# Attention scores as two full-height products over stacked query halves, with three fill steps ahead of them

## Chip, core and metric

The kernel runs on one core of a Trainium2 chip. The metric is the device time of one execution in microseconds (us), here the median of several executions. A core has a matrix engine (TensorE, in the profile PE, with its weight loads as PEld), a vector engine (VectorE, DVE), a scalar engine (ScalarE, ACT), a general engine (GpSimd, POOL), and a sync engine that issues most transfers (SyncE, SP). Each engine runs its own instructions in program order and waits for the others by semaphores. POOL issues transfers too, between its other work.

## Reference

Two layers of a hybrid backbone over 512 latent tokens and 256 context tokens of width 1024. Each layer projects its input once, gives the parts to three mixers (a state-space scan, a two-dimensional Fourier mixer and neighbourhood attention with 6 heads of width 64), joins them by one output projection, and ends in a gated feed-forward. The change is in the attention's scores:

```python
def na_latent(q, k, v, kc, vc, rpb):
    ...
        s_win = jnp.einsum('bqhd,bwqkhd->bhqwk', q_row, k_win).astype(jnp.float32) * scale + bias[None]
        s_win = s_win.reshape(B, H, GRID_W, nwin)
        s_ctx = jnp.einsum('bqhd,bchd->bhqc', q_row, kc).astype(jnp.float32) * scale
        p = jax.nn.softmax(jnp.concatenate([s_win, s_ctx], axis=-1), axis=-1).astype(q.dtype)
    ...

def na_context(qc, kc, vc):
    ...
    s = jnp.einsum('bqhd,bkhd->bhqk', qc, kc).astype(jnp.float32) * d ** -0.5
```

Queries and keys of the latent tokens are rotated by their grid position before. The context's own attention (`na_context`) is needed in the first layer only.

## The kernel before

Every float32 matrix product is done as three products of halves: a value is split into a high part (a rounded copy) and a low part (the rest), and high·high, high·low and low·high are added up in PSUM. Names that end in h and l, or the indices 0 and 1, are the two halves.

**Layer.** The input projection (`w_in`, L600) fills tiles for the scan, the Fourier mixer and, through `rope` (L697 on), rotated queries and keys, which SP writes to DRAM as `qd` and `kd` (head row, half, token). Beside it runs the state-space scan (`ssm`), in 12 units per layer: a scan on DVE (L746), products with tables on POOL (L749 to L759), output products on PE (L768 to L773). Then comes the value projection (`w_v`, L648), and then attention woven with a fill.

**Attention** works on three pairs of heads. `attn_load` (L939) brings in a pair's keys `kt` (128 rows: two heads of 64; both halves; 768 tokens), its queries `ql` (both halves, 512 latent tokens) and, in the first layer, `qc` (256 context tokens), all by transfers that POOL issues (L946, L947, L951). Two pairs are loaded at once; the third when the second has reached its second step. The queries' buffers are slices of one `u` tile, which the scan's tables use before.

A step is one block of 128 queries of a pair: `scores` (L998 on) calls `both` twice per step, for a window of 256 latent keys and for the 256 context keys; with three products for two heads that makes 12 matmuls of 64 rows by 128 columns with 256 moving columns. In the first layer a fifth step per pair, `scores_ctx`, scores the context queries. So there are 5 steps per pair in the first layer and 4 in the second, 27 in all and 324 such matmuls (L996). The softmax follows on DVE (L1017: add the bias, row minimum; L1041, L281: normalise) and ACT (L1019: exponential). One step later PE transposes the probabilities (L1053, 128x128), ACT copies them back (L1055), and PE multiplies them with the values (L1068 in 128x64 tiles, L1078 for the context).

**Order.** `weave` interleaves attention's generator with a fill by the two numbers that it is given: in both layers the Fourier mixer `fnet` (L860 its small tables, L870 `pz`, L875 `three`, L833 its output) and the gated unit of the scan (`glu`), and in the first layer products with modulation weights too (`mod`, L167, weights by L165). Within that code order a scheduler decides each engine's order ahead of the run. The program's instruction list on an engine is then fixed.

The lines that matter below, before and after the change:

| work | before | after |
|---|---|---|
| scores products | L996 | L1014, L1015 |
| loads of keys / queries / context queries | L947 / L946 / L951 | L956, L962 (low half) / L953 / L968 |
| scan: tables' products on POOL | L749 to L759 | L755 to L765 |
| scan: output products on PE | L768, L771, L773 | L774, L777, L779 |
| fnet: tables, `pz`, `three` | L860, L870, L875 | L866, L876, L881 |
| bias on POOL | L1008 | L1027 |
| transposes / values | L1053 / L1068 | L1072 / L1087 |

Of the kernel before, what the change touches and what calls it, by code (L numbers as in the profile page):

```python
# [8 lines left out]
F32 = mybir.dt.float32  # L9
F32R = mybir.dt.float32r  # L10
# [8 lines left out]
NL, NC = 512, 256  # L19
# [15 lines left out]
class Builder:  # L35
# [59 lines left out]
    def consts(self):  # L95
        nc = self.nc
        self.cols = self.k("cols", [128, 8])
        nc.sync.dma_start(self.cols, self.ap["cols"])
        self.ident = self.k("ident", [128, 128])
        self.nidx = self.k("nidx", [128, 96])  # L100
        self.later = self.k("later", [128, 96])
        self.b0 = [self.k(f"b0{i}", [128, 4, 32]) for i in range(2)]
        self.eye16 = self.k("eye16", [128, 16])
        self.junk = self.k("junk", [128, 512], mybir.dt.bfloat16)
        self.zero = self.k("zero", [1, 128], mybir.dt.bfloat16)
        nc.vector.memset(self.zero, 0.0)
        self.sgn, self.nsgn, self.sgn2pi, self.halfpi = (self.cols[:, i:i + 1] for i in range(4))
        self.mhalf = self.cols[:, 4:5]
        self.qd = [self.dram(f"qd{l}", [NH * HD, 2, NT]) for l in range(DEPTH)]
        self.kd = [self.dram(f"kd{l}", [NH * HD, 2, NT]) for l in range(DEPTH)]  # L110
        self.ud = [self.dram(f"ud{l}", [G, HC, 8, 128]) for l in range(DEPTH)]
        self.zd = [self.dram(f"zd{l}", [G, HC, 8, 96]) for l in range(DEPTH)]
        self.tabd = [self.dram(f"tabd{l}", [NU, 2, 128, 1792]) for l in range(DEPTH)]
        self.wd = [self.dram(f"wd{l}", [NU, 128, 240]) for l in range(DEPTH)]
        self.gd = [self.dram(f"gd{l}", [4, DM]) for l in range(DEPTH)]
        self.rbd = [self.dram(f"rbd{l}", [NH, 16, 8, 384]) for l in range(DEPTH)]
        self.xd = [self.dram(f"xd{l}", [6, 128, DM]) for l in range(3)]
        self.decay = {}
        self.turn = [self.k(f"turn{l}", [128, 48]) for l in range(DEPTH)]
        self.rho = [self.k(f"rho{l}", [128, 48]) for l in range(DEPTH)]  # L120
        self.mcol = [[self.k(f"mc{l}{a}", [128, 2, 16]) for a in range(3)] for l in range(DEPTH)]
        self.gcol = [self.k(f"gcol{l}", [128, 2, 8]) for l in range(DEPTH)]
        self.amod = [[self.k(f"am{l}{i}", [128, 2, 8]) for i in range(2)] for l in range(DEPTH)]
        self.dcol = [self.k(f"dcol{l}", [128, NU]) for l in range(DEPTH)]
# [564 lines left out]
        self.fh[j], self.fl[j] = self.split2(eo, pc)  # L689

    def ev_q(self, l, j, pl, pc):
        self.rope(l, lambda i: self.qd[l][128 * j:128 * j + 128, i], pl, pc, -HD ** -0.5)

    def ev_k(self, l, j, pl, pc):
        self.rope(l, lambda i: self.kd[l][128 * j:128 * j + 128, i], pl, pc, 1.0)

    def rope(self, l, dst, pl, pc, scale):  # L697
        nc = self.nc
        if self.rc is None:
            self.rc, self.rs = self.s(), self.s()  # L700
            nc.sync.dma_start(self.rc, self.ap["rope"][:, 0, :])
            nc.sync.dma_start(self.rs, self.ap["rope"][:, 1, :])
        q, sh = self.s(), self.s()
        nc.scalar.activation(q, pl, AF.Copy, scale=scale)
        nc.vector.stream_shuffle(sh, q, [(i + 16) % 32 for i in range(32)])
        (nc.vector if l == 0 else nc.gpsimd).tensor_tensor(out=sh, in0=sh, in1=self.rs, op=ALU.mult)
        self.tt(q, q, self.rc, ALU.mult)
        self.tt(q, q, sh, ALU.add)
        parts = [(q, 0, NL)]
        if pc is not None:  # L710
            qc = self.c()
            nc.scalar.activation(qc, pc, AF.Copy, scale=scale)
            parts.append((qc, NL, NT))
        for x, a, b in parts:
            new = self.s if a == 0 else self.c
            hl = (new(F32R), new(F32R))
            self.split(*hl, x)
            for i in range(2):
                nc.sync.dma_start(dst(i)[..., a:b], hl[i].bitcast(F32))


    def ssm_scan(self, l, k, tab):
# [216 lines left out]
    def attn_load(self, l, hp):  # L939

        nc = self.nc
        last = l == DEPTH - 1
        kt = self.tab(F32R, (128, 2, NT))
        rows = slice(128 * hp, 128 * hp + 128)
        ql = self.Q[hp % 2]
        nc.gpsimd.dma_start(ql, self.qd[l][rows, :, 0:NL])  # L946
        nc.gpsimd.dma_start(kt, self.kd[l][rows])  # L947
        qc = None
        if not last:
            qc = self.QC[hp % 2]  # L950
            nc.gpsimd.dma_start(qc, self.qd[l][rows, :, NL:NT])  # L951
        rb = self.z_p.tile([128, 2, 384], F32, tag="z", name="rb")
        for e in range(2):  # L953
            nc.sync.dma_start(rb[:, e, :], self.rbd[l][2 * hp + e].rearrange("c r n -> (c r) n"))
        return kt, ql, qc, rb

    def attn(self, l):


        nc = self.nc  # L960
        last = l == DEPTH - 1
        ua = self.ua = self.ut(F32R)  # L962
        two = lambda a, n: ua[:, a:a + 2 * n].rearrange("p (i n) -> p i n", i=2)
        self.Q = [two(0, NL), two(2 * NL, NL)]
        if not last:
            qc = self.s(F32R)
            self.QC = [two(4 * NL, NC), qc.rearrange("p (i n) -> p i n", i=2)]
        self.extra = [ua[:, 4 * NL:5 * NL]] if last else []  # L968
        self.bm = [self.q() for _ in range(3)]
        for b in self.bm:  # L970
            nc.gpsimd.memset(b[:, 256:512], 0.0)
        self.mask = [self.c() for _ in range(3)]
        for ty in range(3):
            nc.sync.dma_start(self.mask[ty], self.ap["mask"][:, ty, :])
        self.kq = {hp: self.attn_load(l, hp) for hp in range(2)}
        steps = [(hp, i) for hp in range(3) for i in range(4 if last else 5)]
        pend = []
        self.nbm = 0
        for hp, i in steps:
            pend.append((hp, i, (self.scores if i < 4 else self.scores_ctx)(l, hp, i)))  # L980
            yield
            if len(pend) > 1:
                self.values(l, *pend.pop(0))
            for r in pend[-1][2]:
                self.normalise(*r)
            if i == 1 and hp == 1:
                self.kq[2] = self.attn_load(l, 2)
            yield
        self.values(l, *pend[0])

    def both(self, sp, q, k, qs, ks):

        for n, (a, b) in enumerate(((0, 0), (0, 1), (1, 0))):
            for e in range(2):
                r = slice(64 * e, 64 * e + 64)
                self.nc.tensor.matmul(sp[e], q[r, a, qs], k[r, b, ks], start=(n == 0), stop=(n == 2))  # L996

    def scores(self, l, hp, i):  # L998
        nc = self.nc
# [276 lines left out]
    def build(self):  # L1276
# [46 lines left out]
        for l in range(DEPTH):  # L1323
            last = l == DEPTH - 1
            self.yh, self.yl = [None] * 8, [None] * 8
            self.fh, self.fl = [None] * 2, [None] * 2
            self.rc = self.rs = None
            self.U = [None] * 3
            w = self.w_in(l, 0, 6, pre if l == 0 else None)
            ahead = (AHEAD0, 3)[l]  # L1330
            tables = (lambda k: self.prep_dir(0, big, k, True, "tt")) if l == 0 else (lambda k: self.tables(1, k))
            tabs = {k: tables(k) for k in range(ahead)}
            for _ in range(3):
                next(w)
            self.weave(self.ssm(l, tabs, tables, ahead), w, 13, 8)
            self.run(self.w_v(l))
            fill = self.fnet(l)
            if l == 0:
                mods = self.chain(self.mod(0, 1, "m", self.q), self.mod(0, 2, "m", self.q))
                fill = self.zip(fill, mods, 11, 18)  # L1340
            fill = self.chain(fill, [None] * (0, 4)[l], self.glu(l))
            self.weave(self.attn(l), fill, *((30, 33) if l == 0 else (24, 15)))
            pre_gu = self.gu_pre(l)
            if l == 0:
                ssm_a = self.scalars_load(1)
            self.w_out(l, self.ap["x"] if l == 0 else self.xd[2])
            if l == 0:
                new = lambda: self.xt1()[:, 0:512]
                self.ffn(l, pre_gu, fill=self.chain(self.prep(1, ssm_a), *(self.mod_ahead(1, a, new) for a in range(3))))
            else:  # L1350
                self.ffn(l, pre_gu, out=self.ap["out"])
# [112 lines left out]
```

## Time and profile before

| | |
|---|---|
| median of 3 runs | 1657.88 us (1656.64 to 1658.67) |
| the profiled execution | 1656.89 us |
| its span in the trace | 1655.1 us |
| mean granted TensorE clock in it | 0.982 of full speed |
| PE busy | 1591.4 us, 96% of the span |
| DVE, ACT, POOL busy | 60%, 40%, 14% |
| scores in the first layer | 237.26 us to about 332 us of the span |
| scores in the second layer | 1172.95 us to 1221 us of the span |

How to read the rows further down: times are us from the span's start. A line such as L996 is a line of the kernel before. In a timeline a row gives a start, a duration and a number of instructions (x12); neighbours of one kind are merged; an idle time before the row stands in brackets with what ended it. Matmuls are pipelined, so a row's duration overlaps the next row's start: what a group costs PE is read from its start to the next group's start. In rows of windows each engine has its busy time, PEclk is the granted TensorE clock as a share of full speed (1.00 is 2.4 GHz and 0.50 is 1.2 GHz), and DMA the mean busy share of the 16 DMA engines.

### The profile page before, as it was taken

What the parts mean: (1) busy time and instruction counts of PE and PEld (TensorE: products, weight loads), DVE (VectorE), ACT (ScalarE), POOL (GpSimd) and SP (SyncE); (2) the same over time, 40 slices, a digit from 0 to 9 for tenths busy, and PEclk for the clock granted to TensorE, in tenths of its full rate; (3) what the DMA queues carried; (4) which work ended last, traced back from release to release, by engine and by line L of the source; (5) the groups of instructions that cost most, each with busy time, mean ns of one, the idle gap of its engine ahead of it and who ended that gap; (6) DMA issues with size and microseconds to landing.
All of it is one profiled execution on the core that took longest, in us unless ns stands there. A gap on an engine that the chain in (4) does not pass through costs nothing. (4 is left out here: it accounts for less than half of the span.)

```text
span 1655.1 us, 23574 instructions
## 1 busy us (share of the span) xinstructions
PE 1591.4 (96%) x9097; PEld 1308.6 (79%) x9097; DVE 995.0 (60%) x1855; ACT 663.8 (40%) x1289; POOL 237.3 (14%) x268
## 2 busy tenths in 40 slices
PE   5998889999999999999999999989999999999997
PEld 1887776678988888778788788879777888888886
DVE  7699976765565656433343357697764534554455
ACT  6556655646556322211221138422564432222222
POOL 1000012002111233000000014375411100000002
PEclk8999899999999999999999999999899999999999
DMA  9444368634133424642524346476713322233222
GB/s 333 145 152 139 88 200 252 234 130 160 65 115 128 146 91 141 207 153 90 191 89 149 135 185 207 159 225 195 227 65 140 129 88 102 77 117 103 86 79 86
DMA packets 101391, 240.08 MB, mean 145 GB/s; under 512 B 25424, under 2 KB 56784, under 8 KB 88480
## 3 DMA queue, kind: packets, MB, share of 16 engines
q1 hardware_dynamic: 97968, 229.93, 40.9%
q0 software_dynamic: 3312, 8.65, 1.7%
q8 instruction: 71, 1.16, 0.3%
q14 instruction: 40, 0.33, 0.1%
HBM read 201.26 MB, written 38.47 MB: 145 GB/s over the span
## 5 line engine op out<-in xcount | busy, mean ns | idle before, releaser
L600 PE MATMUL b<-s,wh 128*128 128x512 f32 (+1 forms) x1856 | 552.0, 377 | 7.0 <-DVE c L572 5.3
L600 PEld LDWEIGHTS b<-s,wh 128*128 128x128 f32 x1856 | 338.4, 190 | 80.4 <-issue 10.2
L600 PE MATMUL b<-s,wl 128*128 128x512 f32 (+1 forms) x928 | 346.7, 375 | 1.5 <-DVE wl L572 1.5
L591 ACT ACTIVATE wh<-wr 128x1024 fp32r<-128x1024 f32 (+4 forms) x184 | 185.3, 1027 | 345.6 <-PE b L600 251.5
L572 DVE TENSOR_TENSOR wl<-wr,wh 128x1024 fp32r<-128x1024 f32 (+4 forms) x184 | 221.3, 1219 | 110.6 <-ACT wh L591 100.8
L284 DVE TENSOR_TENSOR q<-q,b 128x512 f32<-128x512 f32 x180 | 122.8, 685 | 165.7 <-PE b L1192 165.1
L600 PEld LDWEIGHTS b<-s,wl 128*128 128x128 f32 x928 | 175.5, 189 | 32.4 <-DVE wl L572 2.6
L600 PE MATMUL b<-c,wh 128*128 128x256 f32 x944 | 179.3, 285 | 0.3 <-ACT c L591 0.3
L600 PEld LDWEIGHTS b<-c,wh 128*128 128x128 f32 x944 | 151.5, 191 | 5.8 <-ACT c L591 0.5
L287 DVE SCALAR_TENSOR_TENSOR s<-s,b 128x512 f32<-128x512 f32 x88 | 60.3, 685 | 134.2 <-PE b L600 86.9
L1192 PE MATMUL b<-wh,tab 128*128 128x512 f32 x400 | 137.1, 393 | 0.0
L600 PE MATMUL b<-c,wl 128*128 128x256 f32 x472 | 133.2, 284 | 0.0
L1192 PE MATMUL b<-wh,s 128*128 128x512 f32 x384 | 130.1, 392 | 0.0
L600 PEld LDWEIGHTS b<-c,wl 128*128 128x128 f32 x472 | 90.3, 191 | 1.4 <-issue 0.2
L1192 PEld LDWEIGHTS b<-wh,tab 128*128 128x128 f32 x400 | 75.1, 188 | 19.1 <-ACT c L1169 2.5
L1192 PEld LDWEIGHTS b<-wh,s 128*128 128x128 f32 x384 | 72.1, 188 | 19.8 <-issue 2.5
L1192 PE MATMUL b<-wl,tab 128*128 128x512 f32 x200 | 78.4, 392 | 0.0
L1192 PE MATMUL b<-wl,s 128*128 128x512 f32 x192 | 74.8, 390 | 0.0
L1224 POOL TENSOR_TENSOR q<-q,g 128x512 f32<-128x512 f32 x10 | 13.9, 1391 | 366.8 <-ACT junk L522 366.8
L591 ACT ACTIVATE s<-s 128x512 fp32r<-128x512 f32 x43 | 26.9, 627 | 93.9 <-DVE s L287 52.8
L534 POOL TENSOR_TENSOR ss<-ss,cols 128x1 f32<-128x1 f32 x42 | 30.6, 730 | 190.6 <-DVE ss L287 190.0
L1169 ACT ACTIVATE s<-b 128x512 f32<-128x512 f32 x44 | 26.0, 590 | 78.2 <-PE b L600 78.1
(329 smaller groups left out, 2633.6 us busy)
## 6 DMA issues: line engine op xcount, KB each, us to landing
wr<-in_w_gu SPq DMA_DIRECT2D x44, 1024.0 KB
wmod<-in_w_mod SPq DMA_DIRECT2D x46, 512.0 KB
wr<-in_w_down SPq DMA_DIRECT2D x22, 1024.0 KB
wmod<-in_w_mod SPq DMA_DIRECT2D x16, 1024.0 KB
wr<-in_w_in SPq DMA_DIRECT2D x10, 1024.0 KB
u<-in_w_mod SPq DMA_DIRECT2D x18, 512.0 KB
wr<-in_w_out SPq DMA_DIRECT2D x8, 1024.0 KB
tab<-tabd SPq DMA_DIRECT2D x12, 640.0 KB
```

The source lines that it names most:

```text
L284: self.nc.vector.tensor_tensor(out=out, in0=a, in1=b, op=op)
L287: self.nc.vector.scalar_tensor_tensor(out=out, in0=a, scalar=s, in1=b, op0=op0, op1=op1)
L534: nc.gpsimd.tensor_tensor(out=ss[:, 3:4], in0=ss[:, 2:3], in1=self.mhalf, op=ALU.pow)
L572: (eng or self.nc.vector).tensor_tensor(out=lo, in0=x, in1=hi.bitcast(F32), op=ALU.subtract)
L591: ins = self.nc.scalar.activation(hi, x, AF.Copy)
L600: self.nc.tensor.matmul(out, a[k], h[k][v][:, cs], start=(k == 0 and i == 0), stop=(k == 7 and i == 2))
L1169: nc.scalar.activation(tmp[v], gp, AF.Tanh, scale=0.5)
L1192: nc.tensor.matmul(pd, a[v][:, cs], w[:, ds], start=(j == 0 and i == 0), stop=(j == n - 1 and i == 2))
L1224: (nc.gpsimd, nc.vector)[hf].tensor_tensor(out=oo[hf], in0=oo[hf], in1=gates[t // 4][:, hf * 512:(hf + 1) * 512], op=ALU.mult)
```

## The change

It has three parts.

1. **Layout and products.** `qd` becomes one block per head with the 64 high rows above the 64 low rows. A query tile then holds, per head, 128 rows: high on rows 0 to 63, low on rows 64 to 127. The keys' high half is loaded twice, onto rows 0 to 63 and rows 64 to 127, and so is the low half. One full-height matmul with the high keys gives high·high + low·high; a second with the low keys gives high·low + low·low. `both` thus issues 2 matmuls per head with 128 rows where it issued 3 with 64: 8 per step for 12, 216 in all for 324.
2. **Loads.** A pair's keys come by two transfers of 384 KB for the high half (L956) and four for the low half (L962: two of 256 KB into `s` tiles, two of 128 KB into `c` tiles) where there was one of 768 KB. With the queries' loads that makes 7 or 8 transfers per pair for 2 or 3, and 768 KB more.
3. **Order of the code.** Attention's generator yields once after its loads, and three steps of the fill are taken before the weave starts; the weave's numbers go from 30:33 to 30:30 and from 24:15 to 24:12.

```diff
     def ev_q(self, l, j, pl, pc):
-        self.rope(l, lambda i: self.qd[l][128 * j:128 * j + 128, i], pl, pc, -HD ** -0.5)
+
+        base = self.qd[l][2 * j]
+
+        def dst(i, a, b):
+            return bass.AP(tensor=base.tensor, offset=base.offset + i * HD * NT + a,
+                           ap=[[2 * HD * NT, 2], [NT, HD], [1, b - a]])
+        self.rope(l, dst, pl, pc, -HD ** -0.5)
...
         kt = self.tab(F32R, (128, 2, NT))
         rows = slice(128 * hp, 128 * hp + 128)
         ql = self.Q[hp % 2]
-        nc.gpsimd.dma_start(ql, self.qd[l][rows, :, 0:NL])
-        nc.gpsimd.dma_start(kt, self.kd[l][rows])
+        qs = self.qd[l][2 * hp:2 * hp + 2].rearrange("e r n -> r e n")
+        nc.gpsimd.dma_start(ql, qs[:, :, 0:NL])
+        for e in range(2):
+            base = self.kd[l][128 * hp + 64 * e:128 * hp + 64 * e + 64]
+            nc.gpsimd.dma_start(kt[:, e, :], bass.AP(tensor=base.tensor, offset=base.offset,
+                                                    ap=[[0, 2], [2 * NT, HD], [1, NT]]))
+        kl = [self.sc(F32R) for _ in range(2)]
+        for e in range(2):
+            base = self.kd[l][128 * hp + 64 * e:128 * hp + 64 * e + 64]
+            for x, a, b in ((kl[e][0], 0, NL), (kl[e][1], NL, NT)):
+                nc.gpsimd.dma_start(x, bass.AP(tensor=base.tensor, offset=base.offset + NT + a,
+                                               ap=[[0, 2], [2 * NT, HD], [1, b - a]]))
+        kt = (kt, kl)
...
+        yield
         for hp, i in steps:
...
-        for n, (a, b) in enumerate(((0, 0), (0, 1), (1, 0))):
-            for e in range(2):
-                r = slice(64 * e, 64 * e + 64)
-                self.nc.tensor.matmul(sp[e], q[r, a, qs], k[r, b, ks], start=(n == 0), stop=(n == 2))
+        kt, kl = k
+        v, c0 = (0, ks.start) if ks.start < NL else (1, ks.start - NL)
+        for e in range(2):
+            self.nc.tensor.matmul(sp[e], q[:, e, qs], kt[:, e, ks], start=True, stop=False)
+            self.nc.tensor.matmul(sp[e], q[:, e, qs], kl[e][v][:, c0:c0 + 256], start=False, stop=True)
...
-            self.weave(self.attn(l), fill, *((30, 33) if l == 0 else (24, 15)))
+            attn = self.attn(l)
+            for g in (attn, fill, fill, fill):
+                next(g)
+            self.weave(attn, fill, *((30, 30) if l == 0 else (24, 12)))
```

How this moves instructions is shown at three places. In these listings `tab` is a tile of high keys (before: of both halves), `s` and `c` hold low keys in the changed kernel, `u` holds queries (and, in the scan's rows of the second layer, the scan's tables).

PE at the start of the first layer's attention, before:

```order
L860 MATMUL b<-s 128x256 x2
L167 MATMUL b<-wmod,scT 32x512 x8
L860 MATMUL b<-s 128x256 x2
L996 MATMUL b<-tab,u 128x256 x12
L870 MATMUL b<-s 128x256 x3
```

and after:

```order
L866 MATMUL b<-s 128x256 x2
L167 MATMUL b<-wmod,scT 32x512 x8
L866 MATMUL b<-s 128x256 x2
L876 MATMUL b<-s 128x256 x3
L774 LDWEIGHTS zero
L774 MATMUL b<-zero 128x384
L777 MATMUL b<-q 128x96 x4
L876 MATMUL b<-s 128x256
L1014 MATMUL b<-tab,u 128x256
L1015 MATMUL b<-s,u 128x256
```

The first step's scores stand four `pz` matmuls and a scan unit's first four rows later, and a step is 8 matmuls in which high and low keys alternate.

PE at the start of the second layer's attention, before:

```order
L870 MATMUL b<-s 128x256 x23
L870 MATMUL b<-s 1x256 x6
L771 MATMUL b<-q,u 128x96
L773 MATMUL b<-U,q 128x96
...
L875 MATMUL b<-wh,s 128x260 x2
L875 MATMUL b<-wl,s 128x260
...
L875 MATMUL b<-wl,c 128x260
L996 MATMUL b<-tab,u 128x256 x30
```

and after:

```order
L774 LDWEIGHTS zero
L774 MATMUL b<-zero 128x384
L777 MATMUL b<-q,u 128x96 x4
L881 MATMUL b<-wh,s 128x260 x2
...
L881 MATMUL b<-wl,c 128x260
L777 MATMUL b<-q,u 128x96
L779 MATMUL b<-U,q 128x96
...
L1014 MATMUL b<-tab,u 128x256
L1015 MATMUL b<-s,u 128x256
```

The thirty `three` matmuls (L875, now L881) stood between the scan's last output products and the first scores; now they stand ahead of those output products, and the scores follow these directly.

POOL at the same place, before:

```order
L947 DMA tab<-kd_128 128x1536
L754 MEMSET q 128x4
L755 TENSOR_TENSOR q<-q 128x4x95
L947 DMA tab<-kd_128 128x1536
L749 TENSOR_TENSOR q<-q,tab 128x384
...
L759 TENSOR_TENSOR q<-q 128x4x31
L947 DMA tab<-kd_128 128x1536
L946 DMA u<-qd_126 128x2x512 x2
```

and after:

```order
L956 DMA tab<-kd_128 128x1x768 x2
L962 DMA c<-kd_128 128x1x256
L760 MEMSET q 128x4
L761 TENSOR_TENSOR q<-q 128x4x95
L956 DMA tab<-kd_128 128x1x768 x2
L755 TENSOR_TENSOR q<-q,tab 128x384
...
L962 DMA c<-kd_128 128x1x256 x2
L763 MEMSET q 128x4
L764 TENSOR_TENSOR q<-q 128x4x64
L765 TENSOR_TENSOR q<-q 128x4x31
L956 DMA tab<-kd_128 128x1x768 x2
L953 DMA u<-qd_126 128x2x512 x2
```

Two transfers stand inside the last scan unit's products and the keys' loads are two each. Seven more low loads stand about two scan units earlier; the third pair's remaining two come among the bias instructions of the stage.

## Rows read from the trace of the kernel before

**Rows 1.** The page's first part: busy time of each engine.

```profile
PE 1591.4 (96%) x9097; PEld 1308.6 (79%) x9097; DVE 995.0 (60%) x1855; ACT 663.8 (40%) x1289; POOL 237.3 (14%) x268
```

**Rows 2.** Windows: the attention of layer one and two in their undisturbed parts.

```profile
core 0: us, PE busy (x) PEld busy (x) DVE busy (x) ACT busy (x) POOL busy (x), PEclk, DMA share, GB/s
245.00:335.00 90.00, 89.38 (x698) 59.92 (x691) 61.22 (x162) 54.82 (x130) 15.89 (x21) 1.00 0.72 233
1189.60:1228.00 38.40, 38.30 (x330) 30.14 (x330) 27.98 (x80) 26.03 (x61) 8.93 (x12) 1.00 0.21 50
```

**Rows 3.** Timeline of PE: scores, transposes and values in the steady stage.

```profile
248.83 1.32 PE L996 MATMUL b<-tab,u 64*128 64x256 f32 x12
250.08 0.66 PE L1053 MATMUL b<-ident,q 128*128 128x128 f32 x4
250.70 0.97 PE L996 MATMUL b<-tab,u 64*128 64x256 f32 x6
251.60 0.66 PE L1053 MATMUL b<-ident,q 128*128 128x128 f32 x4
252.19 0.97 PE L996 MATMUL b<-tab,u 64*128 64x256 f32 x6
...
319.53 0.98 PE L996 MATMUL b<-tab,u 64*128 64x256 f32 x12
320.44 0.54 PE L1068 MATMUL b<-q,vb 128*64 128x128 f32 x5
...
1201.03 1.09 PE L1053 MATMUL b<-ident,q 128*128 128x128 f32 x8
1202.06 0.97 PE L996 MATMUL b<-tab,u 64*128 64x256 f32 x6
```

**Rows 4.** Timeline of PE: the layers' starts of attention, with full-height groups.

```profile
232.70 3.21 PE L167 MATMUL b<-wmod,scT 128*32 128x512 f32 x16 [2.86 <-ACT va L649]
...
240.24 2.74 PE L870 MATMUL b<-s 128*128 128x256 f32 x21
242.82 0.36 PE L771 MATMUL b<-q 128*128 128x96 f32 x2
...
1161.53 0.33 PE L768 MATMUL b<-zero 1*128 1x384 bf16 x1 [0.90 <-DVE z L287]
...
1167.91 0.48 PE L875 MATMUL b<-wh,s 128*128 128x260 f32 x2
...
1172.03 0.28 PE L875 MATMUL b<-wl,c 1*128 1x260 f32 x1
1172.95 0.97 PE L996 MATMUL b<-tab,u 64*128 64x256 f32 x12 [0.64 <-DMA u<-qd]
1175.74 4.20 PE L996 MATMUL b<-tab,u 64*128 64x256 f32 x18 [1.82 <-DVE am L1017]
```

**Rows 5.** Timeline of POOL: the last scan unit of layer two, then its loads.

```profile
1164.82 0.45 POOL L759 TENSOR_TENSOR q<-q 128x124 f32<-128x124 f32 x1
1165.21 0.60 POOL L947 DMA_DIRECT2D tab<-kd  x1
1168.21 1.43 POOL L946 DMA_DIRECT2D u<-qd  x2 [2.40 <-PE b L773]
```

**Rows 6.** Windows: the stretch at the lower clock in layer two, and transfers around it.

```profile
1175.27:1188.92 13.65, 13.08 (x61) 10.68 (x63) 8.24 (x25) 7.05 (x16) 3.84 (x4) 0.50 0.66 220
1170.00:1180.00 10.00, 7.44 (x48) 6.34 (x47) 9.94 (x24) 5.94 (x13) 5.10 (x7) 0.76 0.97 261
260.00:280.00 20.00, 19.94 (x162) 12.88 (x158) 13.35 (x38) 11.47 (x30) 6.49 (x10) 1.00 0.89 278
```

**Rows 7.** Waits from 225 to 340 us: engine, line, releaser, total us, times, longest.

```profile
POOL q L1008 <- DVE am L1017: 22.6, 5, 8.2
ACT va L649 <- DMA wd<-x: 6.1, 1, 6.1
```

**Rows 8.** Transfers issued from 215 to 240 us: number, size, median us to landing.

```profile
u<-qd POOLq DMA_DIRECT2D x2, 512.0 KB, 7.4
```

More of the change, by code (lines that the diff above doesn't have):

```diff
@@ L108, in consts @@
         self.mhalf = self.cols[:, 4:5]
-        self.qd = [self.dram(f"qd{l}", [NH * HD, 2, NT]) for l in range(DEPTH)]
+        self.qd = [self.dram(f"qd{l}", [NH, 2 * HD, NT]) for l in range(DEPTH)]
         self.kd = [self.dram(f"kd{l}", [NH * HD, 2, NT]) for l in range(DEPTH)]
@@ L691, in ev_q @@
     def ev_q(self, l, j, pl, pc):
-        self.rope(l, lambda i: self.qd[l][128 * j:128 * j + 128, i], pl, pc, -HD ** -0.5)
+        base = self.qd[l][2 * j]
[3 more added lines that the diff above has]
+        self.rope(l, dst, pl, pc, -HD ** -0.5)
     def ev_k(self, l, j, pl, pc):
-        self.rope(l, lambda i: self.kd[l][128 * j:128 * j + 128, i], pl, pc, 1.0)
+        self.rope(l, lambda i, a, b: self.kd[l][128 * j:128 * j + 128, i, a:b], pl, pc, 1.0)
     def rope(self, l, dst, pl, pc, scale):
@@ L718, in rope @@
             for i in range(2):
-                nc.sync.dma_start(dst(i)[..., a:b], hl[i].bitcast(F32))
+                nc.sync.dma_start(dst(i, a, b), hl[i].bitcast(F32))
     def ssm_scan(self, l, k, tab):
@@ L950, in attn_load @@
             qc = self.QC[hp % 2]
-            nc.gpsimd.dma_start(qc, self.qd[l][rows, :, NL:NT])
+            nc.gpsimd.dma_start(qc, qs[:, :, NL:NT])
         rb = self.z_p.tile([128, 2, 384], F32, tag="z", name="rb")
```

## The prediction

> **What bounds the kernel now.** I read the busy times first: PE works 96% of the span, the next engine 60% [rows 1]. Then the two attention stages by windows, for a mean hides what stands there. In the first layer's, from 245 to 335 us, PE is busy 89.38 of 90 us, DVE 61, ACT 55, and the transfers take 0.72 of their engines; in the second layer's, 38.30 of 38.40 us with transfers at 0.21 [rows 2]. So in both stages PE's own work sets the time, and what is taken off PE comes off the end, until something else is late. The exceptions are the two starts: in layer one PE waits 2.86 us at 232.70, and in layer two it waits 0.90, 0.64 and 1.82 us at 1161 to 1176 [rows 4], and then runs 13.65 us at a granted clock of 0.50, which is the level of 1.2 GHz [rows 6]. Waits of the other engines inside the stages cost nothing.
>
> **The products of the scores.** Their price is read from a group's start to the next group's start. Twelve take 250.08 - 248.83 = 1.25 us, six take 251.60 - 250.70 = 0.90 us [rows 3]. Both hold the change of shape at the group's end. In program order the first layer's 180 stand in 26 groups: eight of twelve, nine of six and nine smaller ones with 30 matmuls, for which I take 0.125 each, the middle of 1.25/12 and 0.90/6: 10.0 + 8.1 + 3.8 = 21.9 us. The second layer's 144 are six of twelve, seven of six and one group of thirty at 1.25/12: 7.5 + 6.3 + 3.1 = 16.9 us. Together 38.8 us at the full clock. No row shows a 128-row scores product. The nearest is `pz`, which has the same shape (128 rows, 128 columns, 256 moving columns): 21 in 242.82 - 240.24 = 2.58 us, 0.123 each [rows 4]. The new 120 + 96 = 216 would take 26.6 us. **Saved: 12.2 us** (7.1 and 5.1). The added fourth product (low times low) has no price of its own: it lies in rows that the matmul fills anyway.
>
> **Changes of shape.** Four transposes take 250.70 - 250.08 = 0.62 us ahead of half-height scores, and eight take 1.03 (1201.03 to 1202.06) [rows 3]: four more cost 0.41, so leaving them for another shape costs 0.21. 28 of the 40 scores groups are entered from a full-height group (transposes, Fourier products), and each paid this; after, scores are full-height themselves and it is gone: 28 x 0.21 = 5.9 us. On the other side 19 of the 43 new groups are left for value products or modulation products of another tile shape, and now pay it: 4.0 us. Elsewhere in the stages the new order has two such changes more, 0.4 us. **Net: 1.5 us saved.** PE in sum: 13.7, taken as **13.5 us**. The bounds come from one row: at 319.53 twelve took 0.91 us only [rows 3], since there the two heads' halves overlap. If the fourteen twelves all went so, 14 x 0.34 = 4.8 us of the saving was never there: 9. The upper end, with the 28 exits saved and half of the 19 paid, is 16.
>
> That row also bears on a rule that speaks against this change. The Trainium skill, "TensorEngine Tiling (Array Packing)", Overview, says that a matmul with a contraction of at most 64 can share the array with another one, for up to twice the throughput. By that rule twelve would take the slots of six, 0.74 us, and eight full-height ones 0.98: a loss. The trace agrees in part: the second six of a group of twelve cost 1.25 - 0.90 = 0.35 us, three slots, but six alone take 0.90.
>
> **The start of layer two.** Before, the queries' load is issued at 1168.21, as soon as the scan's last product (L773) has freed the `u` tile [rows 5], and the scores start at 1172.95. Those 4.7 us were filled by thirty `three` matmuls, 1167.91 to 1172.03; only 0.64 of wait was left [rows 4]. In the new order these thirty stand ahead of the scan's last output products, and nothing stands between those and the scores. So the load, some 5.0 us from the last product to its landing, is idle time of PE. Against it go 0.64 itself, the 0.90 at 1161.53 (what PE lacked then, it now reaches four us of work later), and about half of the 1.82 for DVE at 1175.74, because the new DVE order has fewer weight splits right behind the first scores. Ahead of `three` some 0.5 us of wait for its operands appears, whose cover was the scan's products: 5.0 - 0.64 - 0.9 - 0.9 + 0.5 = **+3 us**, from +1.5 (all of the 1.82 goes and `three` waits for nothing) to +6 (the load lands in 7.4 us, as in layer one [rows 8], and 1.82 stays). POOL is no part of it: its last unit ended at 1165.27 [rows 5], and three more transfers ahead (0.60 each by the row of 1165.21) would put that to some 1167, while PE comes to these products only at about 1170. The lower clock I expect again with a like price; if the stretch goes, PE's 13.08 us in it [rows 6] become half, -6.5; if it grows by the longer idle, +2.
>
> **The start of layer one.** ACT waits 6.1 us for a store (`wd`) that shares the transfer engines with the loads of keys and queries [rows 7], and PE waits for ACT (2.86 at 232.70). Now 0.5 MB of low keys in `c` tiles goes ahead, while the other low keys were loaded long before. At 278 GB/s [rows 6] that is 1.9 us of transfers; the store overtakes some: **+0.5 us**, from -1 to +2. That the scores come four `pz` matmuls later costs nothing, since those only change places.
>
> **What costs nothing in between.** The third pair's extra loads stand among POOL's bias instructions; POOL waits there 22.6 us in five waits, up to 8.2 at once, for DVE to free buffers [rows 7], so POOL has slack for six transfers of 0.60. SP issues the same number of stores of queries. The layer's 2.4 MB more take 8.5 us of transfers at 278 GB/s, where 0.28 x 90 = 25 us are free.
>
> **Sum:** -13.5 + 3 + 0.5 = -10 us. The profiled execution took 1656.89 us (span 1655.1), 1 us under the median of 1657.88: it would be 1646.9, and the median **1648 us**. With PE from -9 to -16, the starts from +0.5 to +8, the forecast's own range is 1642 to 1654.
>
> **Rivals.**
> A. The half-height products were cheaper than I price them: all pairs overlap as at 319.53, which the rule above would have. PE saves 9, less 3.5: 1652. For it speaks that one row, against it the 1.25 of the groups of twelve in rows 3. Chance 0.10.
> B. Transfers become the bound in layer one. The stage moved 90 x 233 GB/s = 21 MB; with 1.4 MB more inside it and 278 GB/s [rows 6] this takes 80.5 us, about what PE is left with. If the modulation weights come late, half of the layer's gain goes: 1652. Against it: their ring lies ahead by several steps. Chance 0.10.
> C. The stretch at 1.2 GHz in layer two does not come back, since PE works in another order around it: 1641.5. For it speaks only that the first idle goes; against it, that a longer one comes. Chance 0.08.
> D. Slower: the third pair's low keys come late. Their four loads are queued on POOL between bias instructions that wait for DVE, and the first scores of the pair wait for the last of them. If POOL reaches them one step before, PE stands still for a landing of 5.0 to 7.4 us [rows 5, 8] and pays the lower clock after it, up to 6.5 us (half of 13.08): 12 to 14 us per layer. In one layer alone that ends at 1660 to 1662; in both at 1672 to 1676. It decides from 13.3 us on (the gain of 10 and 3.3 to be seen as slower). Against it: the waits in rows 7 show that POOL is ahead of DVE, and the tiles come free early. Chance 0.14.
> E. The start of layer two costs +9 or more: the load lands late among the output weights' transfers (share 0.97 from 1170 to 1180 [rows 6]), and the lower clock lasts longer. 1654 to 1660. Chance 0.08.
>
> **How the numbers follow.** The forecast has 0.50. About 0.2%, 3.3 us, is what a measurement of this kernel can tell from no change, so faster means under 1654.6. Faster: the forecast 0.50, A and B 0.07 each, C 0.08: 0.72. Same: 0.03 each of A and B, 0.07 of E, 0.01 of D: 0.14. Slower: 0.13 of D, 0.01 of E: 0.14. The range from 1641 to 1659 leaves out most of D, a part of C and a part of E, not quite 2 in 10.
>
> **What would show it.** Right: scores products at some 0.12 us from start to start, eight to a step; transposes next to them at four in 0.41; PE still over 99% busy in both stages, layer one's shorter by about 8 us and layer two's scores starting some 3 us later, behind one idle of about 5 us that the query load ends. Wrong would be: eight products that take 1.2 us; an idle before the third pair's first scores with a transfer of low keys behind it; modulation products that wait for their weights; a start of layer one later by more than 2 us; or a low-clock stretch much longer or shorter than 13.65 us.

## The result, and the profile after

The changed kernel takes 1722.13 us, before 1658.19: a ratio of 1.0395, 95% interval 1.0378 to 1.0412. It is 64 us slower where 10 us less were forecast.

The page of the changed kernel, first its busy times, which answer to [rows 1], then the two queues' shares in the transfers (packets, MB, time as a share of 16 engines):

```profile
PE 1588.8 (92%) x8989; PEld 1309.0 (76%) x8989; DVE 993.1 (58%) x1855; ACT 663.5 (39%) x1289; POOL 263.6 (15%) x298
q1 hardware_dynamic: 97716, 229.93, 40.1%
q0 software_dynamic: 39888, 13.50, 4.6%
```

and the queue that POOL issues on (q0) in the kernel before:

```profile
q0 software_dynamic: 3312, 8.65, 1.7%
```

PE is busy 2.6 us less than before, in a span that is 66 us longer (1721.5 us for 1655.1), so the loss is waits. And while POOL's queue moved 4.85 MB more, about the 4.7 MB that the change's loads add, it needed twelve times as many packets. That is the first sign of what happened.

The waits of PE, grouped by releaser (total us, times, longest), from 150 to 380 us and then from 1090 to 1310 us, around the two attention stages:

```profile
PE b L487 <- DVE u L461: 25.9, 4, 19.3
PE b L1014 <- DMA u<-qd: 10.9, 1, 10.9
PE b L167 <- ACT va L649: 6.3, 1, 6.3
PE b L167 <- DMA wmod<-in_w_mod: 5.9, 3, 3.9
...
PE b L1014 <- DMA u<-qd: 25.6, 1, 25.6
PE b L738 <- DMA tab<-tabd: 13.5, 4, 5.5
```

The longest is the first scores of layer two waiting 25.6 us for the queries; the same in layer one is 10.9. Before, these were 0.64 us [rows 4] and none. The timeline of PE in layer two, which answers to the lower part of [rows 4]:

```profile
1220.25 0.39 PE L779 MATMUL b<-U,q 128*128 128x96 f32 x2
1246.25 0.58 PE L1014 MATMUL b<-tab,u 128*128 128x256 f32 x1 [25.61 <-DMA u<-qd]
1246.63 0.42 PE L1015 MATMUL b<-s,u 128*128 128x256 f32 x1
1246.85 0.41 PE L1014 MATMUL b<-tab,u 128*128 128x256 f32 x1
```

After this idle the matmuls start 0.21 us apart, at a granted clock of 0.50 from 1246.25 to 1253 us. The wait of 19.3 us for `u` in layer one hangs on transfers too: DVE (`x`, L284) waits 15.4 us there for the scan's weights. SP issues their load late, because it first waits for a small store (`wd`) that has nothing to do with the change, as SP's timeline shows:

```profile
183.94 1.72 SPq L495 DMA_DIRECT2D wd<-x  x1
200.41 3.06 SPq L505 DMA_DIRECT2D q<-wd  x4
203.52 0.60 SPq L433 DMA_DIRECT2D x<-in_ssm_bc  x1
```

From the store's issue to the loads behind it (L505) it is 16.5 us, where it was 5.2 before (180.47 to 185.64). The loads of keys and queries land late as well. The list of transfers issued from 150 to 300 us (number, KB each, median us from issue to landing) answers to [rows 8], where the queries took 7.4 us:

```profile
tab<-kd POOLq DMA_DIRECT2D x6, 384.0 KB, 18.5
u<-qd POOLq DMA_DIRECT2D x3, 512.0 KB, 19.7
s<-kd POOLq DMA_DIRECT2D x4, 256.0 KB, 11.5
c<-kd POOLq DMA_DIRECT2D x4, 128.0 KB, 12.4
```

128 KB in 12.4 us is not a matter of bytes. From 189 to 200 us hardly more than one load of keys and one store of queries was under way, and the window (columns as in [rows 2]) reads:

```profile
189.00:200.00 11.00, 11.00 (x73) 10.29 (x72) 7.66 (x16) 6.92 (x18) 0.74 (x1) 1.00 0.14 45
```

A share of 0.14 of 16 engines is about two engines, at 45 GB/s together. Two is also the outermost dimension of the new key loads (`[[0, 2], [2 * NT, HD], ...]`) and of the new stores of queries (`[[2 * HD * NT, 2], [NT, HD], ...]`). From this comes theory S: a transfer is spread over as many engines as its outermost dimension has entries. The rivals: L, the plain load of more bytes, more transfers and another order; and later R, that reading the same rows twice is slow.

### The profile page after: what moved, and what is told of

It is laid out like the page before. It is cut to its first block, busy times and chain, and to the rows that moved or that the text cites. A ratio compares the mean times of both kernels' runs of the same rounds, so it can differ in the third digit from the quotient of the medians.

```text
span 1721.5 us, 23434 instructions
## 1 busy us (share of the span) xinstructions
PE 1588.8 (92%) x8989; PEld 1309.0 (76%) x8989; DVE 993.1 (58%) x1855; ACT 663.5 (39%) x1289; POOL 263.6 (15%) x298
## 3 DMA queue, kind: packets, MB, share of 16 engines
q1 hardware_dynamic: 97716, 229.93, 40.1%
q0 software_dynamic: 39888, 13.50, 4.6%
## 5 line engine op out<-in xcount | busy, mean ns | idle before, releaser
L284 DVE TENSOR_TENSOR q<-q,b 128x512 f32<-128x512 f32 x180 | 122.8, 685 | 165.5 <-PE b L1211 164.9
L167 PE MATMUL b<-wmod,scT 128*32 128x512 f32 x192 | 42.8, 747 | 26.5 <-DMA wmod<-in_w_mod 10.9
L1014 PE MATMUL b<-tab,u 128*128 128x256 f32 x104 | 32.8, 337 | 37.0 <-DMA u<-qd 36.5
```

The costliest lines, as they stand in the source:

```text
L167: nc.tensor.matmul(acc[32 * j:32 * j + 32, :], self.scT[:, k, :], w[:, j, :], start=(k == 0), stop=(k == 7))
L284: self.nc.vector.tensor_tensor(out=out, in0=a, in1=b, op=op)
L1014: self.nc.tensor.matmul(sp[e], q[:, e, qs], kt[:, e, ks], start=True, stop=False)
```

## The form of the transfers, one at a time

These runs measure transfers alone: they bring in other rows than the scores need (128 different rows of keys or queries in place of a copy), in the same number and size. The order of work on the engines stays that of the changed kernel (the form of the stores alone shifts some dozens of PE's 8989 matmuls and a few instructions of ACT and DVE). Key loads of one run of 128 rows:

```diff
-            base = self.kd[l][128 * hp + 64 * e:128 * hp + 64 * e + 64]
-            nc.gpsimd.dma_start(kt[:, e, :], bass.AP(..., ap=[[0, 2], [2 * NT, HD], [1, NT]]))
+            base = self.kd[l][128 * hp:128 * hp + 128]
+            nc.gpsimd.dma_start(kt[:, e, :], base[:, e])
```

and the low loads alike.

> The changed kernel (1722 us), in which each of the 36 key loads names its 128 source rows as one run of 128 instead of twice the same 64. Number, size and place of the loads and every engine's order are the same; odd heads get the other head's key rows, so the scores are of wrong keys. Theory S (spread: a transfer whose outermost dimension is 2 is worked off by two of the 16 transfer engines, row after row, and holds up all that is queued behind it): the key loads land in 5 to 8 us instead of 11 to 18, the wait of 25.6 us for the queries in layer two falls to about 5, that of 10.9 in layer one to under 2; the stores of queries are still of that form. Time 1670 to 1690. Rival L (load of the new plan: 4.7 MB more, 14 more transfers issued by POOL, low keys queued inside the scan's chain, scores without cover): nothing of that changes, 1715 to 1725.

Measured: 1672.07 us, ratio to before 1.0094 (1.0078 to 1.0111). 50 of the 64 us were in the form of the 36 loads. Its landings, in the whole program:

```profile
tab<-kd POOLq DMA_DIRECT2D x12, 384.0 KB, 4.8
s<-kd POOLq DMA_DIRECT2D x12, 256.0 KB, 5.0
c<-kd POOLq DMA_DIRECT2D x12, 128.0 KB, 4.2
```

Stores of one run of 128 rows, with the loads left as they were:

```diff
-                           ap=[[2 * HD * NT, 2], [NT, HD], [1, b - a]])
+                           ap=[[NT, 2 * HD], [1, b - a]])
```

> The changed kernel, in which only the 18 stores of queries name 128 rows in one run (high rows of both heads together, then low rows, so the scores are of wrong queries), while the key loads stay as they are. Theory S: POOL no longer waits 16.5 us for a store in layer one and 8.4 in layer two, and what stood behind the stores on the two engines comes earlier: 5 to 20 us off, 1702 to 1717, with the two waits for queries (25.6 and 10.9) still there. Rival L: 1718 to 1726.

Measured: 1700.95 us, 1.0264 (1.0243 to 1.0285). 21 us were in the stores, a little over the forecast's edge. The queries of layer two still came 25.1 us late there.

Both forms:

> The changed kernel with both: key loads and query stores of 128 rows in one run, all orders the same, scores of wrong keys and queries. Theory S: all of the loss of 64 us was in the form of these transfers, and what is left is the sum that was forecast for the change: 1645 to 1656. Rival L: at best the part of the store waits, 1700 or more. Between 1660 and 1690 both are at work.

Measured: 1654.53 us, 0.9984 (0.9973 to 0.9995). All of the loss is gone, with the same number and bytes of transfers. L falls for the loss. It comes back below for the gain. Taken back alone, the two forms gave 50 and 21 us, together they gave 68, so they cost nearly their sum. Both forms have a hand in PE's wait for the scan's tables in layer two (`tab<-tabd`): 13.5 us in the changed kernel, 12.7 with the loads whole, 9.7 with the stores whole, and 1.9 with both.

The third part of the change by itself, on the kernel before:

```diff
+        yield
         for hp, i in steps:
...
-            self.weave(self.attn(l), fill, *((30, 33) if l == 0 else (24, 15)))
+            attn = self.attn(l)
+            for g in (attn, fill, fill, fill):
+                next(g)
+            self.weave(attn, fill, *((30, 30) if l == 0 else (24, 12)))
```

> The kernel before with the third part of the change alone: attention's first yield, three steps of fill ahead, and the weave's new numbers; products, stores and loads as before. Theory S: nothing of the 64 us is here; the queries' load of layer two stands without cover, 3 to 5 us, 1656 to 1663. Rival L: the order is a large part of the loss, 1675 or more.

Measured: 1658.12 us, 1.0007 (0.9998 to 1.0017): nothing.

## Two engines, four, sixteen

The kernel before with its key loads in the twice form:

```diff
-        nc.gpsimd.dma_start(kt, self.kd[l][rows])
+        nc.gpsimd.dma_start(kt, bass.AP(..., ap=[[0, 2], [2 * NT, HD], [NT, 2], [1, NT]]))
```

> The kernel before with one thing changed: its six key loads of 768 KB read twice the first head's 64 rows, by the form with an outermost dimension of 2, instead of 128 rows in one run (odd heads get wrong keys). Same number, size and order. Theory S: such a load of 64 rows of 6 KB on each of two engines takes 20 us or more where it took 5.5, and both attention starts wait for it: 1670 to 1700. Rival L: 1657, within 3 us.

Measured: 1699.58 us, 1.0245 (1.0222 to 1.0269). Six transfers of another form cost 43 us. Their landings, and those of the queries queued behind them:

```profile
tab<-kd POOLq DMA_DIRECT2D x6, 768.0 KB, 23.8
u<-qd POOLq DMA_DIRECT2D x6, 512.0 KB, 19.4
```

Then the changed kernel with other outermost dimensions in its key loads. Twice 64 rows, 127 of the 128 different:

```diff
-ap=[[0, 2], [2 * NT, HD], [1, NT]]
+ap=[[63 * 2 * NT, 2], [2 * NT, HD], [1, NT]]
```

> The changed kernel, whose key loads read 64 rows and then 64 rows from 63 rows further on (so 127 different rows), still with an outermost dimension of 2; all orders the same, wrong keys. Theory S (spread over two engines): as the changed kernel, 1715 to 1728, landings of 11 to 19 us. Rival R (reading the same rows twice is what is slow): near the run with whole rows, 1665 to 1680, landings of 5 us.

Sixteen times the same 8 rows (`ap=[[0, 16], [2 * NT, 8], [1, NT]]`):

> The changed kernel, whose key loads read sixteen times the same 8 rows, an outermost dimension of 16; all orders the same, wrong keys. Theory S: all 16 engines work, 8 rows each, no padding packets: landings of about 5 us, 1667 to 1680 as with whole rows. Rival R: the rows are read sixteen times, landings as long as in the changed kernel or longer, 1715 or more.

Measured: 1723.67 us, 1.0403 (1.0385 to 1.0421), for the first, and 1677.90 us, 1.0127 (1.0107 to 1.0147), for the second. Different rows are as slow as the same, and the same rows read sixteen times are nearly as fast as whole rows. R falls. The landings of the high keys, distinct rows and then sixteen:

```profile
tab<-kd POOLq DMA_DIRECT2D x12, 384.0 KB, 18.7
```

```profile
tab<-kd POOLq DMA_DIRECT2D x12, 384.0 KB, 7.0
```

Four times 32 rows (`ap=[[0, 4], [2 * NT, 32], [1, NT]]`):

> The changed kernel, whose key loads read four times 32 rows (an outermost dimension of 4) instead of twice 64; stores as in it, all orders the same, wrong keys. Theory S: four engines work on each load, the landings halve from 11 to 18 us to some 6 to 9, and the time falls between the changed kernel's 1722 and the 1672 of whole rows: 1680 to 1700. Rival R (what is slow is reading the same rows again, not the spread): no shorter landing, 1715 or more.

Measured: 1722.33 us, 1.0391 (1.0366 to 1.0416). The time did not fall at all, against the expectation, though the landings did in part: the low keys' 256 KB 10.3 us for 14.0, the high keys 17.9 for 19.4, the low keys' 128 KB not (13.2 for 12.9). Layer one's scores started 8 us sooner (265.59 for 273.17) and its stage took 7 us longer. Over the whole program the scores' waits for queries fell from 36.5 to 17.3 us, but other waits of PE grew: those for `va` (L649) from 6.3 to 14.3, those for modulation weights from 10.9 to 15.9. Why is open. That the time goes down with the number of engines is thus not shown between two and four; only that sixteen nearly cure it.

The packets of POOL's queue count the engines. The changed kernel, with an outermost dimension of 2, needed 39888 (above). These are the lines of the run with whole key loads, of that with four and of that with sixteen:

```profile
q0 software_dynamic: 7632, 13.37, 2.9%
```

```profile
q0 software_dynamic: 21456, 13.43, 5.2%
```

```profile
q0 software_dynamic: 7632, 13.37, 3.5%
```

39888 - 7632 = 32256 = 36 loads x 14 engines x 64 packets. 21456 - 7632 = 13824 = 36 x 12 x 32. With sixteen there are none. This is what comes out if each idle engine gets one packet for each of the 64 (or 32) rows that a working engine moves: 13.50 - 13.37 = 0.13 MB for 32256 is 4 bytes each. The Trainium skill, "DMA: Bandwidth & Descriptors", Rules for kernel authors, states the rule: an outermost dimension of c under 16, "e.g. a leading zero-stride broadcast of c copies", confines the transfer to at most c engines. The trace agrees, by these counts and by the share of 0.14. It was to be read off the diff, and the prediction didn't.

SP's queue counts them for the stores, the other way round: 97968 packets before and in the runs with whole stores, 97716 in the changed kernel, 252 fewer = 18 stores x 14. All 252 are of 4 bytes, so a store in that form has 14 such packets less than a whole one.

## Where the forecast gain went

With both forms whole, 2.3 us were gained and not 10. The new products alone, on the tiles, the loads and the code order of before (the products mix the rows of two heads, so this measures their time alone, and the scheduler's order on the engines shifts with them):

```diff
-        for n, (a, b) in enumerate(((0, 0), (0, 1), (1, 0))):
-            for e in range(2):
-                r = slice(64 * e, 64 * e + 64)
-                self.nc.tensor.matmul(sp[e], q[r, a, qs], k[r, b, ks], start=(n == 0), stop=(n == 2))
+        for e in range(2):
+            for b in range(2):
+                self.nc.tensor.matmul(sp[e], q[:, e, qs], k[:, b, ks], start=(b == 0), stop=(b == 1))
```

> The kernel before with the new products alone: two full-height matmuls per head and block (8 per step) on the tiles of before, with the old loads, stores and order of code (the products mix the two heads, so the scores are wrong). Theory P (the forecast of 13.5 us for PE holds, and it is the new loads and order that use it up): 1642 to 1650, 8 to 14 us under before. Rival Q (PE's saving was over-priced, or the chain through DVE and ACT takes its place): 1653 to 1658.

Measured: 1648.12 us, 0.9948 (0.9935 to 0.9961): 10.6 us under the median of the runs of before beside it (1658.75), and 6.5 to 10.8 by the interval. With the third part too:

> The same with the third part too (three fill steps ahead, new weave numbers), still without the new loads and stores, wrong scores. Theory P with the order as the cost: 3 to 5 us slower than the products alone. With the loads as the cost: within 2 us of it.

Measured: 1644.42 us, 0.9926 (0.9910 to 0.9942): 14.3 us under it, and 9.6 to 14.9 by the interval. By the medians this is 3.7 us faster than the products alone, which neither expectation had. The two intervals overlap, so that the third part helps here is likely and not shown; that it costs 3 to 5 us is refuted. These times hold waits too; PE's busy time, 1591.4 us before [rows 1], tells the saving by itself. It fell by 14.7 and 11.9 us, around the 13.5 that were forecast:

```profile
PE 1576.7 (96%) x8989; PEld 1298.8 (79%) x8989; DVE 993.3 (60%) x1855; ACT 662.1 (40%) x1289; POOL 237.1 (14%) x268
```

```profile
PE 1579.5 (96%) x8989; PEld 1303.2 (79%) x8989; DVE 993.7 (60%) x1855; ACT 663.4 (40%) x1289; POOL 237.9 (14%) x268
```

The timeline of PE in the run with the third part answers to [rows 3]:

```profile
256.61 1.22 PE L996 MATMUL b<-tab,u 128*128 128x256 f32 x8
257.66 0.60 PE L1053 MATMUL b<-ident,q 128*128 128x128 f32 x4
...
260.16 0.66 PE L1053 MATMUL b<-ident,q 128*128 128x128 f32 x4
260.57 0.72 PE L996 MATMUL b<-tab,u 128*128 128x256 f32 x4
```

Eight take 1.05 us, entered from value products of another shape, where twelve took 1.25; the prediction had 0.98 for eight. Four transposes ahead of full-height scores take 0.41, as it said, where they took 0.62.

So some 12 us lie between the 14.3 gained here and the 2.3 gained with both forms whole (medians against the runs of before beside them, 1658.75 and 1656.79). They are the price of the new loads in their good form, 4.7 MB more and 30 more instructions on POOL, together with the order that the scheduler gives the engines around these loads, which is another one. The waits of PE in the latter run, layer one and then layer two:

```profile
...
PE b L167 <- DMA wmod<-in_w_mod: 4.5, 1, 4.5
PE b L167 <- ACT va L649: 2.9, 1, 2.9
...
PE b L1011 <- DMA u<-qd: 4.4, 1, 4.4
PE b L738 <- DMA tab<-tabd: 1.9, 1, 1.9
```

The run with products and fill has neither the first nor the third of these (0.5 us for the queries). The third is the lost cover, which was forecast at 5.0. It belongs to the order that comes with the loads: in the run with products and fill, and in that of the third part alone, the thirty `three` matmuls still stand between the scan's last output products and the first scores. The first is the sign of rival B: modulation weights come late. These are the windows from 255 to 290 us, with the loads, and then without them:

```profile
255.00:290.00 35.00, 29.69 (x223) 17.70 (x221) 18.58 (x53) 16.26 (x42) 9.78 (x15) 0.90 0.92 295
```

```profile
255.00:290.00 35.00, 33.70 (x292) 23.18 (x292) 24.62 (x67) 21.77 (x58) 9.19 (x13) 1.00 0.89 281
```

PE is idle for 5.3 us of the first, and runs part of the rest at the lower clock (0.90 in the mean). The transfers' share is nearly the same, 0.92 and 0.89. To see whether the bytes of the third pair's low keys make the weights late:

```diff
+        if l == 0 and hp == 2:
+            kl = self.kq[1][0][1]
```

> The run with both forms whole (1654.5), without the four low-key loads of layer one's third pair (0.75 MB; its scores use the second pair's low keys). If the 4.5 us of wait for modulation weights and the low clock behind it come from these bytes, which travel at a transfer share of 1.0, that wait is gone or under 2 us and the time 1646 to 1651. If it comes from PE running ahead of the weights' ring, the wait stays and the time is 1653 to 1656.

Measured: 1654.21 us, 0.9980 (0.9967 to 0.9993), and the wait is still 4.0 us. So it isn't these bytes. What the timelines show is another order on PE. With both forms whole, two groups of modulation products stand with nothing between them:

```profile
269.25 1.06 PE L167 MATMUL b<-wmod,scT 128*32 128x512 f32 x8
274.81 1.93 PE L167 MATMUL b<-wmod,scT 128*32 128x512 f32 x8 [4.50 <-DMA wmod<-in_w_mod]
```

SP had issued the load of weights that PE waits for at 266.79, and PE was ready for it 3.5 us later. In the run with products and fill the load of that place was issued at 262.35, and the groups stand at 264.85 and 269.56 with other products between them: 7.2 us, and no wait. The run without the third pair's low keys has its two groups side by side too. So it is likely PE's order that brings PE to the weights too soon, but no run changes this order alone, and it is not shown.

## Each twice load as two of 64 rows

Each twice load becomes two transfers of 64 rows, and so does each store of queries:

```diff
-            nc.gpsimd.dma_start(kt[:, e, :], bass.AP(..., ap=[[0, 2], [2 * NT, HD], [1, NT]]))
+            for d in range(2):
+                nc.gpsimd.dma_start(kt[64 * d:64 * d + 64, e, :], base[:, 0])
```

> The change done so that every transfer names 64 or 128 rows in one run: each duplicated key load is two loads of 64 rows, each store of queries two of 64 rows. 36 more loads on POOL and 18 more stores on SP. Theory S: as the run with whole rows (1654.5), the extra instructions of 0.55 us on POOL and SP lie beside other work: 1648 to 1657. If the number of transfers counts for itself (rival L), 1660 or more.

Measured: 1668.86 us, 1.0074 (1.0062 to 1.0087). The form is good, but there are too many. POOL now issues 13 loads per pair, and at the start of layer two, where it works on the scan's tables, three stretches of four loads, 2.1 us each, stand in its way. The scan's products on PE wait for it (waits of PE from 1090 to 1260 us):

```profile
PE b L779 <- POOL q L767: 6.3, 1, 6.3
PE b L1016 <- DMA u<-qd: 4.8, 1, 4.8
PE b L776 <- DVE z L287: 4.0, 2, 2.3
```

The forecast had POOL's extra issues as free. They were for 3 more in that chain, and are not for this many. The same without the third part of the change:

> The same without the third part: no fill steps ahead, the old weave numbers. In the whole-row run 4.5 us of wait for modulation weights and then a low clock stood in layer one, and 5 us at the start of layer two. If these come from the third part, this is 4 to 8 us faster than the run before it, 1642 to 1650; if they come from the transfers and the scheduler, it is within 3 us of it.

Measured: 1676.23 us, 1.0113 (1.0094 to 1.0132), 7 us slower, which neither branch of the expectation had: the third part is no cause of the loss here; without it things are worse.

With both heads' high keys in one load of 64 rows for each half of the partitions, and a pair's six low loads on SP or on POOL:

> A correct version with fewer and moved transfers: one load of 64 rows brings the high keys of both heads (two per pair), the low keys go by six loads of 64 rows on SP instead of POOL, stores of queries of 64 rows. POOL then issues 4 to 5 loads per pair where the split version has 13 to 14. Theory S with the count on POOL as the rest of the loss: POOL no longer holds the scan's chain (6.3 us of PE wait in the split version) and the Fourier products stand ahead of the scores again: 1640 to 1652. If the split version's 1669 came from the store form of 64 rows or from SP: 1660 or more.

> The same with the six low loads on POOL, so 10 to 11 loads per pair there. If the count on POOL is what the split version lost by, this lies between: 1652 to 1666.

Measured: 1658.12 us, 1.0008 (0.9997 to 1.0018), and 1659.36 us, 1.0010 (0.9998 to 1.0022). Fewer loads, 9 per pair with the queries' for 13, win 10 us back. The first run stayed above its forecast of 1640 to 1652: whether six of the loads sit on POOL or SP is the same within 2 us, so the count on POOL is not the rest. The stores left whole, the stacking done at the load instead, with and without the third part:

> A correct version: queries stored whole as before (128 rows, no added stores), their stacking done at the load by two loads of 64 rows, high keys by two loads of 64 rows for both heads, low keys by six loads of 64 rows on SP. PE's saving is the one of the products with fill (14 us), against it the 4.7 MB more: if the added stores held up e11 (1658), 1646 to 1654; if the added bytes and loads do, 1655 to 1660.

> The same without the third part (old weave numbers, no fill ahead). The products alone were 4 us faster with the fill than without, so 2 to 5 us slower than the run before it; if the transfers of the first pair are late without the fill ahead, more.

Measured: 1660.94 us, 1.0029 (1.0019 to 1.0040), and 1665.21 us, 1.0042 (1.0028 to 1.0056). The first should have come to 1654 or less if the added stores had held these versions up, so they alone were not what did. None of these beat the kernel before: in every version that was tried, loading the keys onto both halves costs about what full height saves, or more.

## Why the prediction was wrong

- **The step that failed** is the price of the new loads and stores. In "What costs nothing in between" they were priced by bytes (2.4 MB at 278 GB/s) and by issue (0.60 us), with landings taken from rows of transfers of one run of 128 rows [rows 8]. The new ones have another form, which no row of before showed, and the prediction says nothing of it: it took 7.4 us for the latest landing. Measured: landings of 11 to 20 us from 150 to 300 us, two engines of 16 at work, and a loss of 64 us that goes when the form goes (1654.53). The stores of queries were dismissed as "the same number"; their form cost 21 us.
- **Rival E** had the right place, a queries' load that lands late at the start of layer two, but made it +9 us for want of that price; it was 25.6 of wait. **Rival D**, the slow mechanism with 0.14, named the third pair, whose scores waited for no keys. That the forecast and its rivals all missed is thus one omission, not bad luck.
- **PE**: 13.5 us forecast; 14.7 and 11.9 us less busy time measured, 10.6 us of time alone and 14.3 with the new order. Right, by its own steps. Rival A's 9 us for PE are too few by these, and lie just outside the interval of the run with the third part (9.6 to 14.9). The loss that the prediction worked out for half-height products at their best did not come: the products alone were faster, at 1648.12 us.
- **The start of layer two**: 5.0 us of uncovered load forecast, 4.44 measured once the form was whole. Right in mechanism and size. The start of layer one, forecast at +0.5, was then as before: PE waited 2.9 us for ACT.
- **Rival B**'s sign did come, 4.5 us of wait for modulation weights with both forms whole, and about the 4 us that it would take. Its mechanism, transfers as the bound, is not shown: the wait stayed with 0.75 MB less. Against it the prediction said that the weights' ring of buffers lies ahead by several steps; there it did not, as the load at 266.79 shows.
- **The range**: by its own terms (PE -9, the starts +8) the upper end is 1657 and not 1654. The measured time is far outside either.
- **Rival C** had half a point: the stretch at the lower clock in layer two was shorter in the whole-row run, though a longer idle preceded it: a mean of 0.70 over 11.30 us of this window (columns as in [rows 2]) is 6.8 us at 0.50 and the rest at 1.00, where it was 13.65 us at 0.50 [rows 6].

```profile
1178.70:1190.00 11.30, 10.82 (x66) 9.57 (x66) 7.45 (x23) 6.83 (x17) 3.30 (x5) 0.70 0.74 210
```

## What to carry to other kernels

Read the outermost dimension of every transfer that a change adds or rewrites before its bytes: here two entries meant two engines of 16 and four meant four, and transfers that shared these engines were held back. A copy onto two partition halves was better as two transfers of 64 rows (1668.86 us for 1722.13), but each costs its issue, so count them on the issuing queue. And measure a saving on the bound engine apart from the data movement that it needs: here it stood at 10 to 14 us, and the movement, with the order that came with it, ate it.

## What the hardware showed

Not expected: POOL's queue has a packet of 4 bytes for every idle engine and every row that a working engine moves (64 x 14 = 896 per load of the changed kernel). The SP queue has none of these; a store in that form has 14 packets less than a whole one (97968 before and 97716 after, for 18 stores), and these stores cost 21 us all the same. And transfers on two engines delay others far from them: from a store of 120 KB to SP's next loads it was 16.5 us where it had been 5.2, and the scan's weights, whose load came behind them, were awaited for 15.4 us.
